# A decoder trunk on one core: attention's written order laid out anew, rsqrt in eleven steps, products by twos

## The chip, the cores and the metric

The kernel runs on one core of a Trainium2 chip. The metric is the device time of one execution in microseconds (us); for a set of runs the median is given. The engines are TensorE (matmuls, called PE in the profile, its weight loads PEld), VectorE (DVE), ScalarE (ACT), GpSimd (POOL) and SyncE (SP), which issues the DMAs. Each engine works through its own queue in order and waits for others by semaphores.

## The reference, cut to what matters

A trunk of two layers on 256 tokens with a model width of 1024, all in float32. `ffn` is a SwiGLU of hidden width 2816, `rms` an RMS norm:

```python
h = h + 0.5 * ffn(rms(h)); h = h + short_conv(rms(h)); h = h + 0.5 * ffn(rms(h))   # layer 0
k_c, v_c, k_s, v_s, k_w, v_w = shared_kv(h)                                       # one K/V for layer 1
h = h + 0.5 * ffn(rms(h)); h = h + nsa(rms(h), kv); h = h + 0.5 * ffn(rms(h))      # layer 1

def nsa(x):                              # 16 heads of 64 in 4 groups
    q = rms(x @ w_q)                     # per head: q / sqrt(mean(q*q) + 1e-6)
    g = sigmoid(x @ w_g)                 # three gates per head
    # softmax attention over compressed blocks, selected blocks and a window
    return (g0 * o_compressed + g1 * o_selected + g2 * o_window) @ w_o
```

## The kernel before, in words

Activations lie transposed: 1024 features as 8 chunks of 128 partitions, 256 tokens along the free dimension. To keep float32 accuracy every weight tile and every activation is split into a high part and a low remainder in the type fp32r. ACT makes the high part by a copy (L148, "uh" in attention), DVE or POOL the low part by a subtraction (L165, "ul"). A weight block of 128 x 128 then needs two matmuls, which form a pair: the high block against 512 columns (high and low activations side by side; L320 and L429), and the low block against the 256 high columns (L322 and L431). The two halves are added when the result leaves PSUM.

The weights stream through SBUF by DMA in pieces of 128 x 2048. A piece is two units, a unit is 8 blocks. At most six split units are ahead of TensorE.

**FFN, first half** (`ffn_in`): 22 groups of hidden features; in each, gate and up are 8 pairs each, 16 pairs in all. **FFN, second half** (`out_proj`): 8 output columns of 22 pairs each. The order of the pairs is set by a run length: with run r, TensorE does r high products, then their r low products, and so on. `RUNS = (1, 2, 4, 8)` gives group f the run length RUNS[f % 4], and likewise column c; the convolution's groups (24 pairs), the first group of an FFN that has to wait for its norm, and the attention's output projection use run 1.

**Attention** has 16 heads, worked on as 8 pairs of heads p. Its instructions are issued in an order written out by hand: `ORDER` is a list of words, each the name of an operation, with the engine behind a colon where there is a choice (D is DVE, A is ACT, P is POOL). The words are issued from left to right, each engine takes its own in that order, and the order between engines is only what data and buffers ask for. The words that matter here:

- `qHT.k` are the query matmuls of half H of the heads and tile T of the tokens, six matmuls each (L810 to L812). `qsq`, `qsum`, `qrec` make the inverse RMS per head: for H = 0 by a square root on ACT and a reciprocal on DVE, for H = 1 by an iteration without a square root (`q_newton`, L842 to L855), one word with 19 small instructions on 128 x 8 elements. `qrr` multiplies in the token's scale (L860), `qnrm` normalizes the query (DVE, L866), `qtr` transposes it (TensorE, L875), `qput` puts it back into SBUF.
- `S0p`, `S0cp`, `S1p` are the scores of pair p. They take banks of PSUM from a ring of two (tag "mm"). `A0`, `M0`, `U0`, `A1`, `E1` add the bias, take the extreme value and the exponential with its sum, `R` and `W` make the factor (L1026, L1029), `N0` and `N1` multiply it in (POOL, L1032 and L1036, 128 x 512 each), `X` transposes the result (L1045), `C` copies it to SBUF, `PV` multiplies by the values, `Oh` and `Ol` split the output. `cmn` to `cC` are the same for the compressed blocks of two pairs of heads.
- `woC.k` are pieces of the output projection for chunk C (L1186 calls `a_pass`), `wv` adds it to the residual (DVE, L1194), `nh` and `nl` write the high and the low half of the next FFN's input (ACT L268, DVE L272), `ns` squares the chunk and adds it up for the next norm, both on POOL (L285, L288, L289).

A word `uh` that finds no free unit, and a word `ul` that finds no high part waiting, issues nothing.

Of the kernel before, what the change touches and what calls it, by code (L numbers as in the profile page):

```python
# [37 lines left out]
ORDER = """
    q00.0 q00.1 q00.2 norm_pe q00.3 norm_act:A q01.0 norm_dve:D qsq00:A qsum00:D q01.1 uh6:A qsqrt00:A ul6:D q01.2 uh7:A qrec00:D ul7:D qrr00:P q01.3
    uh8:A qnrm00:D gates_pe qsq01:A ul8:D qsum01:D cb0:P qtr00 gates_sum:D qsqrt01:A q10.0 qput00:A cb1:P qrec01:D qrr01:P qnrm01:D cb2:P gates_mm S00  # L40
    gates_exp:A qtr01 cb3:P A00:D q10.1 qput01:D cb4:P M00:D S0c0 cb5:P gates_end:D U00:A S10 cb6:P cx0:D q10.2 A100:D cb7:P A101:D E100:A q10.3 E101:A
    S01 S0c1 qsq10:A A01:D S11 R0:D cx1:D W0:P qsum10:D q11.0 N00:P M01:D qrec10:P cmn0:D U01:A A110:D X00 S02 C00:D S0c2 q11.1 A111:D E110:A cx2:D A02:D
    S12 E111:A N101:P M02:D q11.2 A120:D N100:P U02:A R1:D A121:D qrr10:P X10 csub0:P X20 W1:P qnrm10:D q11.3 N01:P cexp0:A C20:A csum0:D C10:D E120:A
    N110:P crec0:D qtr10 X01 qsq11:A cg0:P qput10:D S03 N111:P C01:A qsum11:D S0c3 E121:A S13 cx3:D cmul0:P A03:D qrec11:P cT0 cmn1:D uh9:A M03:D X21 X11
    cC0:D C21:A S05 R2:D ul9:D C11:A PV0 U03:A A05:D A130:D W2:P qrr11:P PV1 N121:P qnrm11:D Oh0:A E130:A N120:P A131:D qtr11 Ol0:D Oh1:A N02:P X12 E131:A
    M05:D X22 Ol1:D csub1:P S04 qput11:D C12:A X02 R3:D C22:A A04:D W3:P S0c4 N130:P C02:A S0c5 cx4:D M04:D cexp1:A S15 U05:A N131:P cx5:D csum1:D cmn2:D
    S14 crec1:D A150:D cg1:P N03:P X23 U04:A A140:D X13 csub2:P X03 A151:D cmul1:P cT1 A141:D S06 C23:A cC1:A S0c6 C03:D C13:A S16 E141:A cx6:D A06:D PV2
    M06:D E140:A A160:D D06:P PV3 E150:A R4:D A161:D W4:P N141:P cexp2:A Oh2:A csum2:D S07 E151:A N140:P Ol2:D crec2:D S17 A07:D N04:P Oh3:A R5:D M07:D
    X14 E06:A S0c7 E160:A Ol3:D cg2:P X04 W5:P C14:D cmul2:P X24 N05:P cx7:D C04:A U06:D cT2 wo0.0 C24:A cC2:D N151:P cmn3:D E161:A A170:D PV4 N150:P
    A171:D uh10:A csub3:P R6:D E170:A X25 ul10:D W6:P D07:P X05 X15 C25:A C05:D N06:P wo1.0 uh11:A C15:D N161:P X06 cexp3:A ul11:D E07:A PV5 C06:A N160:P  # L50
    Oh4:A csum3:D U07:D E171:A Ol4:D X26 crec3:D cg3:P X16 Oh5:A R7:D C26:D uh12:A cmul3:P wo2.0 W7:P Ol5:D N170:P C16:D uh13:A cT3 wo1.1 ul12:D N171:P
    cC3:A uh14:A wo0.1 ul13:D N07:P X17 ul14:P X27 C17:A X07 C27:D PV6 C07:A PV7 Oh6:A Ol6:D wo0.2 Oh7:A wo2.1 Ol7:D wo0.3 wo2.2 wv0:D uh15:A wo2.3 wo1.2
    wv2:D wo1.3 ns0:P nh0:A wo3.0 uh16:A ul15:P nl0:D wv1:D wo4.0 nh2:A uh17:A ul16:D ns1:P wo3.1 nh1:A nl2:D wo3.2 ul17:D wo3.3 ns2:P wo5.0 uh18:A wv3:D
    wo4.1 ul18:P uh19:A nl1:D wo4.2 nh3:A ul19:D wo4.3 wo5.1 uh20:A ns3:P nl3:D wo5.2 wv4:D uh21:A wo5.3 ul20:P wo6.0 wv5:D nh4:A uh22:A ul21:D wo7.0
    ns4:P nh5:A wo7.1 nl4:D nl5:D ul22:D wo6.1 ns5:P wo6.2 wo6.3 wo7.2 wv6:D wo7.3 wv7:D ns6:P nh6:A nl6:D nh7:A nl7:D ns7:P
"""


# [1 line left out]
def trunk(ctx, tc, A, out):  # L60
# [199 lines left out]
    class Norm:  # L260
# [22 lines left out]
        def square(self, c):  # L283
            if c == 0:
                po.tensor_tensor(out=self.sq, in0=h[c], in1=h[c], op=ALU.mult)  # L285
            else:
# [2 lines left out]
                po.tensor_tensor(out=self.sq, in0=self.sq, in1=s, op=ALU.add)  # L289
# [24 lines left out]

    def a_pass(o, u, xs, ks, last=7, run=1):

        ks = list(ks)
        for i in range(0, len(ks), run):
            for k in ks[i:i + run]:
                pe.matmul(o, u[0][:, k * P:(k + 1) * P], xs[k], start=(k == 0), stop=False)  # L320
            for k in ks[i:i + run]:
                pe.matmul(o[:, :T], u[1][:, k * P:(k + 1) * P], xs[k][:, :T], start=False, stop=(k == last))  # L322
# [458 lines left out]
    X = {}  # L781
# [57 lines left out]
            ve.reciprocal(X["r", hf, tt], s)  # L839
        return fn  # L840

    def q_newton(hf, tt):  # L842
        def fn(e):
            s = X["s", hf, tt]
            y, z = sm([P, 8]), sm([P, 8])
            e.tensor_scalar(out=s, in0=s, scalar1=1.0 / 64, scalar2=EPS, op0=ALU.mult, op1=ALU.add)
            e.tensor_scalar(out=y.bitcast(I32), in0=s.bitcast(I32), scalar1=-0.5, scalar2=float(0x5f3759df), op0=ALU.mult, op1=ALU.add)
            e.tensor_scalar(out=s, in0=s, scalar1=-0.5, scalar2=None, op0=ALU.mult)
            for _ in range(4):
# [3 lines left out]
                e.tensor_tensor(out=y, in0=y, in1=z, op=ALU.mult)  # L853
            X["r", hf, tt] = y
        return fn  # L855

    def q_rr(hf, tt):
        def fn(e):
            r = X["r", hf, tt]
            e.tensor_scalar(out=r, in0=r, scalar1=rq[:, tt:tt + 1], scalar2=None, op0=ALU.mult)  # L860
# [426 lines left out]
```

## Time and profile before

| | |
|---|---|
| median of 3 runs | 1000.1 us |
| the three runs | 997.15, 1000.1, 1002.04 us |
| the profiled execution | 997.46 us |
| its span, first to last instruction | 995.7 us |
| mean granted TensorE clock | 0.998 |
| busy in the span | PE 979.1, DVE 742.6, ACT 558.1, POOL 188.2 us |
| attention, first query matmul to the rows matmul of the last FFN | 703.0 to 811.8 us |
| the other stages begin at | FFN 6, its projection 136, convolution 198, FFN 288, its projection 413, shared K/V 475, FFN 509, its projection 641; after attention the last FFN, its projection 930 |

Times in the profile count from the start of the span. A row of the timeline gives the start, the length, the engine, the line, the operation with output and inputs, the count, and in brackets how long the engine had been idle and what ended that. A row of a group gives, behind the bar, the busy time in us and the mean length of one instruction in ns, then the idle time before them and what ended it. Matmuls overlap in TensorE's pipeline, so their lengths add up to more than the time between their starts.

### The profile page before, as it was taken

To read this page: it belongs to the slowest core of one execution; us is meant where nothing else is said; L and a number is where in the kernel's file an instruction comes from. 1 tells how busy PE (TensorE), PEld (TensorE's weight loads), DVE (VectorE), ACT (ScalarE), POOL (GpSimd) and SP (SyncE) were. 2 spreads that over 40 slices of the span, in tenths; PEclk is the share of its full clock that TensorE was granted. 3 is DMA by queue.
4 is the path that set the end of the run, shared out by engine and by line. 5 is a ranking of instruction groups with operands and counts; after the bars stand their busy time and mean duration, and the time that the engine had idled before them with its cause. 6 is when DMAs were issued, how large, how long until landed. Compare 5 with 4: busy or idle time off the path is not lost.

```text
span 995.7 us, 14600 instructions
## 1 busy us (share of the span) xinstructions
PE 979.1 (98%) x5672; PEld 840.2 (84%) x5672; DVE 742.6 (75%) x1059; ACT 558.1 (56%) x897; POOL 188.2 (19%) x278
## 2 busy tenths in 40 slices
PE   8999999999999999999999999999998989999998
PEld 6888888888888888888888888888866778888887
DVE  6987775568898787877559988866568798787752
ACT  4766554455456655554456667644578556655530
POOL 5000001134460000011011031011368750000000
PEclk9999999999999999999999999999999999999999
DMA  7755565545645655555634556564800445555550
GB/s 241 257 184 200 176 212 182 199 133 207 201 150 209 198 183 186 201 206 169 201 137 153 192 205 219 204 212 160 254 19 4 152 148 206 197 183 187 200 185 22
DMA packets 28721, 177.59 MB, mean 178 GB/s; under 512 B 3259, under 2 KB 6587, under 8 KB 7916
## 3 DMA queue, kind: packets, MB, share of 16 engines
q1 hardware_dynamic: 28652, 176.66, 52.3%
q8 instruction: 44, 0.72, 0.3%
q14 instruction: 25, 0.20, 0.1%
HBM read 175.57 MB, written 1.08 MB: 177 GB/s over the span
## 4 chain that ended last, share of the span: by engine, by line
PE 91%; POOL 4%; DVE 2%; issue 2%; DMA 1%; SPq 0%; ACT 0%; DVEq 0%; POOLq 0%; ACTq 0%
PE mm L320 36%; PE mm L322 18%; PE a L429 17%; PE a L431 9%; PE a L320 2%; POOL pr L1036 1%; PE a L539 1%; PE a L541 1%; PE a L540 1%; PE a L322 1%; DVE xs L272 1%; POOL t L1032 1%; DMA hall<-in_x_dram 1%; DVE wl L165 1%; DVE hall L1194 1%
## 5 line engine op out<-in xcount | busy, mean ns | idle before, releaser
L320 PE MATMUL mm<-xs,wh 128*128 128x512 f32 x1536 | 474.5, 398 | 5.3 <-DVE xs L272 2.8
L165 DVE TENSOR_TENSOR wl<-ws,wh 128x1024 fp32r<-128x1024 f32 x318 | 399.1, 1258 | 84.8 <-ACT wh L148 73.2
L148 ACT CAST wh<-ws 128x1024 fp32r<-128x1024 f32 x322 | 335.7, 1045 | 85.8 <-PE a L429 60.2
L322 PE MATMUL mm<-xs,wl 128*128 128x256 f32 x1536 | 316.9, 281 | 0.8 <-DVE wl L459 0.8
L320 PEld LDWEIGHTS mm<-xs,wh 128*128 128x128 f32 x1536 | 268.0, 189 | 49.7 <-DVE xs L279 3.9
L322 PEld LDWEIGHTS mm<-xs,wl 128*128 128x128 f32 x1536 | 262.1, 189 | 28.1 <-DVE wl L459 1.3
L429 PE MATMUL a<-act,wh 128*128 128x512 f32 x722 | 216.5, 395 | 0.0
L431 PE MATMUL a<-act,wl 128*128 128x256 f32 x722 | 141.7, 280 | 0.0
L429 PEld LDWEIGHTS a<-act,wh 128*128 128x128 f32 x722 | 124.2, 188 | 17.7
L431 PEld LDWEIGHTS a<-act,wl 128*128 128x128 f32 x722 | 121.5, 189 | 14.3
L332 DVE TENSOR_TENSOR t<-mm,t 128x512 f32<-128x512 f32 x96 | 66.1, 688 | 76.7 <-ACT t L331 76.1
L331 ACT COPY t<-mm 128x512 f32<-128x512 f32 x96 | 56.1, 584 | 102.9 <-PE mm L322 102.9
L347 ACT ACTIVATE t<-t 128x256 f32<-128x256 f32 x88 | 36.8, 419 | 63.7 <-DVE t L336 63.6
L336 DVE TENSOR_TENSOR t<-t,R 128x512 f32<-128x512 f32 x88 | 61.6, 700 | 2.8
L288 POOL TENSOR_TENSOR t<-hall 128x256 f32<-128x256 f32 x42 | 35.6, 847 | 137.6 <-DVE hall L398 128.6
L285 POOL TENSOR_TENSOR sq<-hall 128x256 f32<-128x256 f32 x6 | 3.7, 615 | 301.5 <-DVE hall L398 294.8
L325 ACT CAST act<-t 128x256 fp32r<-128x256 f32 x96 | 39.0, 407 | 28.3 <-DVE t L493 19.3
L278 ACT ACTIVATE xs<-hall,gains 128x256 fp32r<-128x256 f32 x40 | 19.7, 505 | 53.9 <-DVE hall L398 49.9
L398 DVE SCALAR_TENSOR_TENSOR hall<-a,hall 128x256 f32<-128x256 f32 x78 | 32.9, 422 | 17.9 <-PE a L431 14.9
L326 DVE TENSOR_TENSOR act<-t,act 128x256 fp32r<-128x256 f32 x96 | 41.0, 427 | 4.3 <-ACT act L325 4.3
L348 DVE TENSOR_TENSOR t<-t,t 128x256 f32<-128x256 f32 x88 | 36.9, 420 | 4.0 <-ACT t L347 4.0
L279 DVE SCALAR_TENSOR_TENSOR xs<-hall,gains,xs 128x256 fp32r<-128x256 f32 x40 | 27.1, 687 | 15.7 <-ACT xs L278 15.7
(233 smaller groups left out, 837.5 us busy)
## 6 DMA issues: line engine op xcount, KB each, us to landing
ws<-in_ffn_w_in_dram SPq DMA_DIRECT2D x86, 1024.0 KB, 4.9
ws<-in_ffn_w_out_dram SPq DMA_DIRECT2D x44, 1024.0 KB, 4.8
ws<-in_conv_w_in_dram SPq DMA_DIRECT2D x12, 1024.0 KB, 4.7
ws<-in_w_kv_dram SPq DMA_DIRECT2D x6, 1024.0 KB, 4.9
ws<-in_conv_w_out_dram SPq DMA_DIRECT2D x4, 1024.0 KB, 4.8
ws<-in_attn_w_q_dram SPq DMA_DIRECT2D x4, 1024.0 KB, 4.8
ws<-in_attn_w_o_dram SPq DMA_DIRECT2D x4, 1024.0 KB, 9.8
...
```

Source lines behind the costliest of these rows:

```text
L148: ac.copy(h, src)
L165: e.tensor_tensor(out=l, in0=src, in1=h.bitcast(F32), op=ALU.subtract)
L320: pe.matmul(o, u[0][:, k * P:(k + 1) * P], xs[k], start=(k == 0), stop=False)
L322: pe.matmul(o[:, :T], u[1][:, k * P:(k + 1) * P], xs[k][:, :T], start=False, stop=(k == last))
L325: ac.copy(dst[:, :T], src)
L326: ve.tensor_tensor(out=dst[:, T:], in0=src, in1=dst[:, :T].bitcast(F32), op=ALU.subtract)
L331: ac.copy(r, o[:, :, T:])
L332: ve.tensor_tensor(out=r, in0=o[:, :, :T], in1=r, op=ALU.add)
L336: ve.tensor_tensor(out=r, in0=r, in1=R[:, None, :].to_broadcast([P, n, T]), op=ALU.mult)
L348: ve.tensor_tensor(out=s, in0=s, in1=r[:, 1], op=ALU.mult)
L429: pe.matmul(o, wh, lhs[k], start=(k == 0), stop=False)
L431: pe.matmul(o[:, :T], wl, lhs[k][:, :T], start=False, stop=(k == n - 1))
```

## The change

1. `RUNS = (2, 2, 2, 2)`, and the default run length of `a_pass` and `a_group` is 2.
2. The iteration for the queries of the second half is rewritten. It works on half the mean square, so that a step is z = y*y, z = z*s, y = (z - 1.5)*y, whose sign flips each time; three rounds are done instead of four, which gives 11 instructions instead of 19. The sign is undone in `qrr`. Each instruction is a word of its own, `qnt1T.i`, with an engine of its own.
3. `ns` is divided: `nq` squares on ACT, `ns` adds on POOL (seven of them, the first square is written in place).
4. `ORDER` is laid out anew, with the lengths of operations taken from a trace. The engine changes in 19 words: all `ul` words are now on DVE (four were on POOL), `qrr10` goes from POOL to DVE, and of the copies `C` and `cC` seven go from DVE to ACT and seven from ACT to DVE.
5. The buffer of the compressed scores of two pairs is made by whichever of the two comes first (`cx`).

```diff
-    RUNS = (1, 2, 4, 8)
-    def a_pass(o, u, xs, ks, last=7, run=1):
+    RUNS = (2, 2, 2, 2)
+    def a_pass(o, u, xs, ks, last=7, run=2):
...
-    def a_group(parts, xs, mid=None, run=1):
+    def a_group(parts, xs, mid=None, run=2):
...
+        def square_by_act(self, c):
+            self.s = getattr(self, "s", {})
+            o = self.sq if c == 0 else t1()
+            ac.activation(o, h[c], AF.Square)
+            self.s[c] = o
+        def add(self, c):
+            po.tensor_tensor(out=self.sq, in0=self.sq, in1=self.s.pop(c), op=ALU.add)
...
-    def q_newton(hf, tt):
+    def q_newton(hf, tt, i):
         def fn(e):
             s = X["s", hf, tt]
...
+            if i == 0:
+                e.tensor_scalar(out=s, in0=s, scalar1=0.5 / 64, scalar2=0.5 * EPS, op0=ALU.mult, op1=ALU.add)
+            elif i == 1:
+                e.tensor_scalar(out=y.bitcast(I32), in0=s.bitcast(I32), scalar1=-0.5, scalar2=float(0x5f3759df - (1 << 22)),
+                                op0=ALU.mult, op1=ALU.add)
+            elif i % 3 == 2:
                 e.tensor_tensor(out=z, in0=y, in1=y, op=ALU.mult)
+            elif i % 3 == 0:
                 e.tensor_tensor(out=z, in0=z, in1=s, op=ALU.mult)
-                e.tensor_scalar(out=z, in0=z, scalar1=1.5, scalar2=None, op0=ALU.add)
-                e.tensor_tensor(out=y, in0=y, in1=z, op=ALU.mult)
-            X["r", hf, tt] = y
+            else:
+                e.scalar_tensor_tensor(out=y, in0=z, scalar=1.5, in1=y, op0=ALU.subtract, op1=ALU.mult)
```

The new list, in the stretch of the first iteration, in that of the second, at the last pairs, and at the end:

```
... A02:D W1:P E101:A N01:P qsum10:D S12 cx2:D E100:A N110:P qnt10.0:D M02:D qnt10.1:D q11.1 U02:A qnt10.2:D R0:D N111:P qnt10.3:D
A120:D qnt10.4:D A121:D W0:P qnt10.5:P q11.2 N100:P E120:A qnt10.6:D qnt10.7:D qnt10.8:D qnt10.9:D N101:P E121:A qnt10.10:D q11.3
qrr10:D qnrm10:D N00:P R2:D qtr10 qsq11:A W2:P cT0 N02:P qput10:D X20 cC0:A S03 qsum11:D C20:A N121:P S05 uh9:A A03:D S0c3 X10
qnt11.0:D N120:P cx3:D M03:D uh10:A X00 S13 C10:D qnt11.1:P C00:A qnt11.2:P cmn1:D qnt11.3:P A05:D csub1:P U03:A X11 qnt11.4:D
A130:D PV0 qnt11.5:P qnt11.6:P qnt11.7:D C11:D qnt11.8:P cexp1:A qnt11.9:P E130:A csum1:D qnt11.10:D A131:D qrr11:P X01 Oh0:A X21
qnrm11:D uh11:A S04 C01:D qtr11 ...
... N170:P wo0.1 cmul3:P ul12:D X17 wo1.1 C17:A N07:P cT3 X27 ul14:D cC3:A X07 C27:A PV6 C07:A ul11:D ul13:D PV7 ...
... wo7.0 nl5:D uh22:A wv6:D ns4:P wo7.1 ul18:D nq6:A nh6:A wo7.2 wo7.3 ns5:P wv7:D ns6:P nq7:A nl6:D nh7:A ns7:P nl7:D ul20:D ul21:D ul22:D
```

More of the change, by code (lines that the diff above doesn't have):

```diff
@@ L38 @@
 ORDER = """
[L39 to L54, printed above, removed]
@@ new lines @@
+    U01:A csub0:P S10 A110:D q10.3 cexp0:A A111:D E110:A csum0:D A100:D E111:A S02 crec0:D A101:D cg0:P S0c2 cmul0:P qsq10:A q11.0 R1:D A02:D W1:P E101:A
+    N01:P qsum10:D S12 cx2:D E100:A N110:P qnt10.0:D M02:D qnt10.1:D q11.1 U02:A qnt10.2:D R0:D N111:P qnt10.3:D A120:D qnt10.4:D A121:D W0:P qnt10.5:P
+    q11.2 N100:P E120:A qnt10.6:D qnt10.7:D qnt10.8:D qnt10.9:D N101:P E121:A qnt10.10:D q11.3 qrr10:D qnrm10:D N00:P R2:D qtr10 qsq11:A W2:P cT0 N02:P
+    qput10:D X20 cC0:A S03 qsum11:D C20:A N121:P S05 uh9:A A03:D S0c3 X10 qnt11.0:D N120:P cx3:D M03:D uh10:A X00 S13 C10:D qnt11.1:P C00:A qnt11.2:P
@@ new lines @@
+    S06 Oh2:A Ol3:D E151:A S0c6 Ol2:D S16 cg2:P A06:D N140:P R5:D X04 M06:D cmul2:P X24 cx6:D C04:A A160:D W5:P X14 D06:P C24:A S07 A161:D C14:A S0c7
+    N05:P E06:A cT2 A07:D S17 E161:A cC2:D N151:P U06:D PV4 E160:A M07:D N150:P cx7:D A170:D uh14:A D07:P R6:D A171:D X05 Oh4:A X15 E170:A Ol4:D W6:P
+    N06:P X25 C05:D wo0.0 C15:A C25:D N161:P E07:A cmn3:D PV5 E171:A U07:D N160:P R7:D W7:P ul10:D csub3:P X16 Oh5:A cexp3:A X26 C16:A N171:P Ol5:D X06
+    C26:A csum3:D wo1.0 crec3:D C06:D cg3:P N170:P wo0.1 cmul3:P ul12:D X17 wo1.1 C17:A N07:P cT3 X27 ul14:D cC3:A X07 C27:A PV6 C07:A ul11:D ul13:D PV7
@@ new lines @@
+    Oh6:A Ol6:D wo1.2 Oh7:A wo0.2 Ol7:D wo2.0 wo1.3 wo0.3 wv1:D uh15:A wo3.0 wv0:D nq1:A wo3.1 nh1:A ul15:D uh16:A wo4.0 nq0:A nl1:D nh0:A ns1:P wo4.1
+    nl0:D wo4.2 ul16:D wo3.2 wo3.3 wo4.3 wv3:D uh17:A wo2.1 wv4:D nq3:A wo2.2 nh3:A wo2.3 ul17:D uh18:A wo5.0 nq4:A wv2:D uh19:A wo6.0 nl3:D nq2:A wo5.1
+    ul19:D nh2:A nh4:A uh20:A wo5.2 nl4:D wo5.3 ns2:P wo6.1 wv5:D uh21:A ns3:P wo6.2 nh5:A wo6.3 nl2:D nq5:A wo7.0 nl5:D uh22:A wv6:D ns4:P wo7.1 ul18:D
+    nq6:A nh6:A wo7.2 wo7.3 ns5:P wv7:D ns6:P nq7:A nl6:D nh7:A ns7:P nl7:D ul20:D ul21:D ul22:D
@@ L840, in q_rec @@
         return fn
-    def q_newton(hf, tt):
+    def q_newton(hf, tt, i):
         def fn(e):
             s = X["s", hf, tt]
[L845 to L849, printed above, removed]
+            if i == 0:
+                X["y", tt], X["z", tt] = sm([P, 8]), sm([P, 8])
+            y, z = X["y", tt], X["z", tt]
+            if i == 0:
+                e.tensor_scalar(out=s, in0=s, scalar1=0.5 / 64, scalar2=0.5 * EPS, op0=ALU.mult, op1=ALU.add)
[3 more added lines that the diff above has]
+            elif i % 3 == 2:
                 e.tensor_tensor(out=z, in0=y, in1=y, op=ALU.mult)
+            elif i % 3 == 0:
                 e.tensor_tensor(out=z, in0=z, in1=s, op=ALU.mult)
-                e.tensor_scalar(out=z, in0=z, scalar1=1.5, scalar2=None, op0=ALU.add)
-                e.tensor_tensor(out=y, in0=y, in1=z, op=ALU.mult)
-            X["r", hf, tt] = y
+            else:
+                e.scalar_tensor_tensor(out=y, in0=z, scalar=1.5, in1=y, op0=ALU.subtract, op1=ALU.mult)
         return fn
@@ L858, in fn @@
         def fn(e):
-            r = X["r", hf, tt]
-            e.tensor_scalar(out=r, in0=r, scalar1=rq[:, tt:tt + 1], scalar2=None, op0=ALU.mult)
+            if hf:
+                r = X["r", hf, tt] = sm([P, 8])
+                e.tensor_scalar(out=r, in0=X["y", tt], scalar1=rq[:, tt:tt + 1], scalar2=-1.0, op0=ALU.mult, op1=ALU.mult)
+            else:
+                r = X["r", hf, tt]
+                e.tensor_scalar(out=r, in0=r, scalar1=rq[:, tt:tt + 1], scalar2=None, op0=ALU.mult)
         return fn
@@ L903, in trunk @@
             else:
-                add(f"qrec{n}", q_newton(hf, tt))
+                for i in range(11):
+                    add(f"qnt{n}.{i}", q_newton(hf, tt, i))
             add(f"qrr{n}", q_rr(hf, tt))
@@ L1077, in cx @@
         def cx(e):
-            if i2 == 0:
+            if ("cm", m) not in X:
                 X["cm", m] = mk([P, 2, 2, 2, 16], "cm", 2)
@@ L1205, in trunk @@
         add(f"nl{c}", lambda e, c=c: nm2.low(c))
-        add(f"ns{c}", lambda e, c=c: nm2.square(c))
+        add(f"nq{c}", lambda e, c=c: nm2.square_by_act(c))
+        if c:
+            add(f"ns{c}", lambda e, c=c: nm2.add(c))
     W.limit, W.cap = NBUF, 1 << 20
```

8 lines of the change are left out of this document (7 added, 1 removed).

## The prediction

> **What bounds the kernel now.** I read the page's chain that ended last first, then the busy time of each engine stage by stage (the rows with two times: length, then PE, weight loads, DVE, ACT and POOL), then TensorE's timeline, and last the rows of the engines that it waits for.
>
> ```profile
> PE 91%; POOL 4%; DVE 2%; issue 2%; DMA 1%; SPq 0%; ACT 0%; DVEq 0%; POOLq 0%; ACTq 0%
> ...
> 785.10:802.80 17.70, 17.43 (x100) 15.01 (x99) 15.18 (x20) 9.08 (x13) 13.33 (x10) 1.00 0.42 147
> 802.80:811.80 9.00, 6.20 (x33) 4.53 (x31) 8.82 (x11) 4.18 (x5) 8.23 (x9) 1.00 0.44 157
> 703.00:811.80 108.80, 99.73 (x681) 75.58 (x679) 83.33 (x196) 69.81 (x184) 76.45 (x137) 1.00 0.36 113
> ```
>
> TensorE's matmuls are 91% of the chain, so outside attention only a shorter matmul stream can help. Attention, from the first query matmul at 703.0 to the rows matmul of the last FFN at 811.8, is the exception: TensorE is idle 108.80 - 99.73 = 9.07 us there, 2.8 of them in the last 9 us. These are its five waits above one microsecond:
>
> ```profile
> 736.10 1.09 PE L1045 MATMUL a<-small,pr 128*128 128x128 f32 x8 [1.78 <-POOL pr L1036]
> ...
> 748.39 0.63 PE L875 MATMUL a<-small,t 128*128 128x128 f32 x4 [1.68 <-DVE t L866]
> ...
> 780.83 0.66 PE L1045 MATMUL a<-small,t 128*128 128x128 f32 x4 [1.10 <-POOL t L1032]
> ...
> 805.46 0.47 PE L320 MATMUL mm<-xs,wh 128*128 128x512 f32 x1 [1.10 <-DVE xs L272]
> ...
> 808.36 0.50 PE L320 MATMUL mm<-xs,wh 128*128 128x512 f32 x1 [1.50 <-DVE xs L272]
> ```
>
> Together 7.16 us; 1.91 lie in smaller ones. The first three end when POOL lets something go (the second through DVE, which had waited for the query scale of POOL), the last two when DVE writes a low half of the normalized input.
>
> **Part 1, runs of two.** All groups now take two high products, then two low ones. The price is read where nothing else moves, between group starts of the first FFN, and between output columns:
>
> ```profile
> 90.92 0.40 PE L320 MATMUL mm<-xs,wh 128*128 128x512 f32 x1
> 96.54 0.40 PE L320 MATMUL mm<-xs,wh 128*128 128x512 f32 x1
> ...
> 124.56 0.40 PE L320 MATMUL mm<-xs,wh 128*128 128x512 f32 x1
> 130.22 0.40 PE L320 MATMUL mm<-xs,wh 128*128 128x512 f32 x1
> 135.81 0.40 PE L429 MATMUL a<-act,wh 128*128 128x512 f32 x1
> 143.58 0.40 PE L429 MATMUL a<-act,wh 128*128 128x512 f32 x1
> 151.26 0.40 PE L429 MATMUL a<-act,wh 128*128 128x512 f32 x1
> 158.96 0.40 PE L429 MATMUL a<-act,wh 128*128 128x512 f32 x1
> 166.62 0.40 PE L429 MATMUL a<-act,wh 128*128 128x512 f32 x1
> ...
> 212.02 0.40 PE L320 MATMUL a<-xs,wh 128*128 128x512 f32 x1
> 220.50 0.40 PE L320 MATMUL a<-xs,wh 128*128 128x512 f32 x1
> ```
>
> Columns of 22 pairs take 7.77, 7.68, 7.70 and 7.66 us at runs of 1, 2, 4 and 8: 0.09 in four, eight columns in three projections (0.54) and seven in the last (0.2). Groups of 16 pairs take 5.66 us at run 1 (from 124.56), 5.59 at run 2 (130.22) and 5.62 at run 4 (90.92); run 8 by the columns is 7.66 x 16 / 22 = 5.57. Four groups gain 0.07 + 0.03 - 0.02 = 0.08; an FFN has 22, so 0.45, and four FFNs 1.8. A convolution group has 24 pairs at run 1, 8.48 us; at 5.59 / 16 a pair it is 8.39, eight times 0.09 = 0.7. The short projections of convolution and attention have about 50 pairs that join a run of two, at 0.07 / 16 each: 0.2. Sum **-3.4 us**. TensorE is busy all through these stages, so nothing hides it.
>
> The Trainium skill ("TensorE: Matmul & The Clock Gate", sections "LDWEIGHTS (loading the stationary operand)" and "Back-to-back issue gap") gives 128 / 1.2 = 107 ns for a weight load and 256 / 2.4 + 2.5 = 109 ns for the shorter matmul. By it every load is hidden in any order and this term would be zero; the trace disagrees, by the differences above.
>
> **Part 2, the rsqrt iteration.** Before, one word puts 19 dependent steps on POOL in one block, twice.
>
> ```profile
> 728.67 0.20 POOL L846 TENSOR_SCALAR sm<-sm 128x8 f32<-128x8 f32 x1
> ...
> 733.84 0.20 POOL L853 TENSOR_TENSOR sm<-sm,sm 128x8 f32<-128x8 f32 x1
> 734.00 2.04 POOL L1036 TENSOR_TENSOR pr<-pr,sm 128x512 f32<-128x512 f32 x2
> ...
> 740.89 0.20 POOL L846 TENSOR_SCALAR sm<-sm 128x8 f32<-128x8 f32 x1
> ...
> 742.54 1.03 POOL L853 TENSOR_TENSOR sm<-sm,sm 128x8 f32<-128x8 f32 x1
> ...
> 746.86 0.20 POOL L853 TENSOR_TENSOR sm<-sm,sm 128x8 f32<-128x8 f32 x1
> ...
> 742.34 1.17 DVE L165 TENSOR_TENSOR wl<-ws,wh 128x1024 fp32r<-128x1024 f32 x1
> ```
>
> The first holds POOL's queue 5.4 us (18 spacings of 0.287), and the products that X10 waits 1.78 us for stand right behind it; the second holds it 6.2 us, and the 1.68 is behind that one. Now there are 11 steps, in the first chain ten on DVE and one on POOL, in the second four and seven. POOL loses 38 steps and gets 8; DVE gets 14 and a scale.
>
> A 128x8 step has no row on DVE. The nearest is the reciprocal of that size, 187 ns (below); POOL's 287 ns is the other end for an undisturbed one. I take 187. But the row at 742.54 shows a third price: a 128x8 POOL step took 1.03 instead of 0.20 while DVE ran a weight split (742.34 to 743.51) that reads two SBUF tiles. The reverse happens at 788.70: DVE's split, 0.48 us alone, ended 0.29 after POOL's.
>
> ```profile
> L1026 DVE RECIPROCAL sm<-sm 128x8 f32<-128x8 f32 x8 | 1.5, 187 | 0.0
> ...
> L866 DVE TENSOR_TENSOR t<-a,sm 128x512 f32<-128x512 f32 x4 | 2.8, 692 | 5.5 <-POOL sm L860 5.5
> L279 DVE SCALAR_TENSOR_TENSOR xs<-hall,gains,xs 128x256 fp32r<-128x256 f32 x1 | 0.5, 483 | 0.6 <-ACT xs L278 0.6
> ...
> 788.70 2.63 DVE L272 SCALAR_TENSOR_TENSOR xs<-hall,gains,xs 128x256 fp32r<-128x256 f32 x1
> ...
> 788.64 2.40 POOL L165 TENSOR_TENSOR wl<-ws,wh 128x1024 fp32r<-128x1024 f32 x1
> ...
> 732.66 0.50 PE L810 MATMUL a<-wh,xs 128*128 128x512 f32 x1
> ...
> 733.92 0.40 PE L812 MATMUL a<-wl,xs 128*128 128x512 f32 x1
> ```
>
> In the new list, after the POOL step of the first chain, TensorE has q11.2 and q11.3 left before the transposes of that query tile: 12 matmuls at (733.92 - 732.66) / 5 = 0.25, 3.0 us. Opposite stand steps 6 to 10 on DVE, while POOL does N100, N101 and N00, 1.02 each, without a gap. Undisturbed: 0.29 + 5 x 0.187 + 0.19 (scale) + 0.69 (normalization) = 2.1, covered with 0.9 to spare. If steps 6, 7 and 8 each wait for one product: 0.29 + 3.06 + 3 x 0.19 + 0.69 = 4.6, **1.6 us of idle TensorE**, and A- and M-words queued behind on DVE are late too. I take the second, since steps 6 to 10 read two SBUF tiles as the split does. The Trainium skill ("SBUF — State Buffer", section "Who interferes with whom") says that such a DVE instruction contends with a GpSimd one that reads SBUF, and the later fully blocks; it names no size below which it doesn't. The trace agrees at 788.70; no run yet shows it for a small DVE step.
>
> In the second chain POOL itself waits for DVE's steps, so no product stands in between: 7 x 0.287 + 4 x 0.187 = 2.8 instead of 6.2. The 1.68 goes.
>
> **Part 3, the other moves.** All weight splits go to DVE, squares of the attention output's norm to ACT; POOL keeps seven adds there.
>
> ```profile
> L165 DVE TENSOR_TENSOR wl<-ws,wh 128x1024 fp32r<-128x1024 f32 x318 | 399.1, 1258 | 84.8 <-ACT wh L148 73.2
> L347 ACT ACTIVATE t<-t 128x256 f32<-128x256 f32 x88 | 36.8, 419 | 63.7 <-DVE t L336 63.6
> ...
> L165 POOL TENSOR_TENSOR wl<-ws,wh 128x1024 fp32r<-128x1024 f32 x4 | 9.8, 2442 | 0.0
> L289 POOL TENSOR_TENSOR sq<-sq,t 128x256 f32<-128x256 f32 x8 | 7.1, 885 | 0.6
> L1194 DVE SCALAR_TENSOR_TENSOR hall<-mm,hall 128x256 f32<-128x256 f32 x8 | 3.3, 420 | 1.3 <-PE mm L322 1.1
> ...
> 778.76 2.02 POOL L1032 TENSOR_TENSOR t<-t,sm 128x512 f32<-128x512 f32 x1
> ```
>
> POOL loses 9.8 us of splits that held DVE up; DVE gains 4 x 1.26. Squares cost ACT 8 x 0.42 = 3.4 (an activation of the same shape), hidden: ACT is busy 9.08 of 17.70. From the last value products TensorE has 52 pairs of the projection and 14 of the FFN, 66 x 0.349 = 23.0 us, before it needs the last low half; DVE starts 2.4 us in and must do 16 x 0.42 + 8 x 0.48 + 5 x 1.26 = 16.9, so 3.7 to spare. Seven adds of 0.885 that each stop DVE cost 6.2, 2.5 too many. Between 0 and 2.5 I take **1.0 left** of 2.6. X07's 1.10 stays: N07 took 2.02 beside a split, and two splits stand beside it again. Of the 1.91 in small waits, which no edit addresses one by one, I leave 0.8, between 0 and all.
>
> **Sum.** Idle left 1.6 + 1.1 + 1.0 + 0.8 = 4.5 of 9.07: **-4.6**. With the runs -8.0. The profiled execution took 997.46 (span 995.7 and 1.8 around it), which makes 989.5; the median of the three runs is 1000.1, 2.6 above it, so I forecast **992.1 us**.
>
> **Rivals.** (a) Small DVE steps aren't stopped, and the tail's cover holds: 1.9 idle left, -10.6, **989.5**. For it: 0.9 to spare. Against: 788.70. (b) The waits only move: each engine's queue is in order, and one late word on DVE delays the scores' evacuation and with it the next scores. Idle again 9, the runs alone, **996.7**. For it: DVE is busy 83 of 108.8 and gets 8 us more. Against: POOL, which ended most waits, loses 9 us of steps (11.6 for 8 x 0.287) and 9.8 of splits. (c) The pair order does nothing: -4.6, **995.5**; against it, columns and groups differ by their run length alone. This is what the rule on weight loads, named above from the Trainium skill, would give. (d) Slower: the mutual stop of DVE and POOL becomes the bound. It lies in the two chains and the tail: 11 two-tile steps of both chains behind 1.02 (11.2), four more splits doubled as at 778.76 (4.2), seven adds (6.2), 21.6 idle instead of 9.07: 1000.1 - 3.4 + 12.5 = **1009**. It decides once idle passes 12.5; against it: in the second chain POOL has nothing else to run.
>
> **How the numbers follow.** My forecast 0.58 (990 to 995), (a) 0.17, (b) 0.17, (c) 0.03, (d) 0.05. A difference below 0.5%, 5 us, can't be told from none here. Faster: forecast and (a), and a third of (b), 0.80; same 0.15; slower 0.05. The range reaches from no idle left (1000.1 - 3.4 - 9.1 = 987.6) and 2 us of the spread of the runs (997.15 to 1002.04) below it, 985.5, to just past (b), 997.5.
>
> **What would show it.** Right: group starts 5.59 apart in every FFN; no wait of X10 for products; DVE steps near 1 us beside POOL's products, and an idle TensorE of 1 to 2 us before the transposes of the third query tile; TensorE busy over 95% from 703 to 802. Wrong: steps all near 0.19 (then (a)); idle of 9 us at other words, the scores' banks above all (b); groups still unequal (c).

## The result and the profile after

The changed kernel takes **990.77 us** in the median of four runs (990.24 to 991.3), the kernel before 1000.52 (997.15 to 1002.04): a ratio of 0.9907, 95% interval 0.9881 to 0.9933. The two profiled executions, 990.75 and 997.46 us, have spans of 988.9 and 995.7.

The page of the kernel after (span, busy times, chain of waits), then its busy times over attention (first query matmul to rows matmul; columns as in the prediction: PE, weight loads, DVE, ACT, POOL, granted clock, DMA share, GB/s):

```profile
span 988.9 us, 14575 instructions
...
PE 976.5 (99%) x5672; PEld 838.3 (85%) x5672; DVE 745.8 (75%) x1078; ACT 560.3 (57%) x905; POOL 163.8 (17%) x235
...
PE 96%; DVE 2%; POOL 1%; issue 0%; DMA 0%; ACT 0%; SPq 0%; POOLq 0%; DVEq 0%; ACTq 0%
```

```profile
701.01:805.85 104.84, 99.83 (x679) 76.65 (x678) 84.06 (x214) 72.05 (x192) 51.64 (x94) 0.98 0.34 108
```

TensorE's share of the chain has grown from 91% to 96%, POOL's has gone from 4% to 1%. In attention TensorE is idle 104.84 - 99.83 = 5.0 us instead of 9.07, but its clock there is 0.98 and not 1.00: something besides waiting has come in. (In before the rows matmul starts at 811.40; the prediction's window went on to 811.80, with no idle time in between. So attention is 108.41 us long here.) These are TensorE's waits in attention above 0.3 us:

```profile
735.53 1.09 PE L894 MATMUL a<-small,t 128*128 128x128 f32 x4 [2.41 <-DVE sm L1046]
...
739.74 0.40 PE L994 MATMUL mm<-KT,wh 64*128 64x16 f32 x4 [0.34 <-DVE t L1003]
...
775.59 0.33 PE L1172 MATMUL a<-small,zp 128*128 128x128 f32 x1 [0.43 <-POOL zp L1167]
777.56 0.66 PE L1065 MATMUL a<-small,t 128*128 128x128 f32 x4 [1.21 <-POOL t L1052]
790.70 0.73 PE L331 MATMUL mm<-act,wh 128*128 128x512 f32 x2 [0.62 <-DVE hall L1214]
```

The first is `qtr10`, the transposes of the third query tile. They read `t`, which the normalization (L885) has written by 735.38; the reciprocal that the profile names stands right behind it in DVE's queue. The 1.21 is `X07`; the last is the second piece of the output projection of chunk 2, which waits for `wv3` to have read its PSUM bank. Of before's five large waits only X07's is left. No wait for a low half (`xs`) remains at the tail.

Stage by stage, between the rows matmuls that follow each norm's squares (and the first query matmul), in us of the two profiled spans:

| stage | before | after | difference |
|---|---|---|---|
| start to first rows matmul | 20.40 | 22.15 | +1.75 |
| FFN 1 and its projection | 184.47 | 183.55 | -0.92 |
| convolution | 89.33 | 88.25 | -1.09 |
| FFN 2, projection, shared K/V | 214.33 | 213.27 | -1.06 |
| first FFN of layer 1 to the first query matmul | 194.45 | 193.79 | -0.66 |
| attention | 108.41 | 104.84 | -3.57 |
| last FFN to the end | 184.27 | 183.10 | -1.17 |

### The profile page after: what moved, and what is told of

Read it like the earlier page. It is cut to its first block, busy times and chain, and to the rows that moved or that the text cites. A ratio compares the mean times of both kernels' runs of the same rounds, so it can differ in the third digit from the quotient of the medians.

```text
span 988.9 us, 14575 instructions
## 1 busy us (share of the span) xinstructions
PE 976.5 (99%) x5672; PEld 838.3 (85%) x5672; DVE 745.8 (75%) x1078; ACT 560.3 (57%) x905; POOL 163.8 (17%) x235
## 4 chain that ended last, share of the span: by engine, by line
PE 96%; DVE 2%; POOL 1%; issue 0%; DMA 0%; ACT 0%; SPq 0%; POOLq 0%; DVEq 0%; ACTq 0%
PE mm L331 37%; PE mm L333 18%; PE a L440 17%; PE a L442 8%; PE a L331 3%; PE a L333 1%; PE a L550 1%; PE a L552 1%; PE a L551 1%; PE a L1065 1%; PE a L821 1%; PE mm L999 1%; PE a L1081 1%; PE a L822 1%; PE a L823 1%; PE mm L990 0%
## 5 line engine op out<-in xcount | busy, mean ns | idle before, releaser
L331 PE MATMUL mm<-xs,wh 128*128 128x512 f32 x1536 | 488.5, 399 | 2.7 <-DVE xs L281 2.2
L333 PEld LDWEIGHTS mm<-xs,wl 128*128 128x128 f32 x1536 | 289.6, 189 | 69.1 <-DVE wl L470 0.8
L333 PE MATMUL mm<-xs,wl 128*128 128x256 f32 x1536 | 304.2, 279 | 0.5 <-DVE wl L470 0.5
L331 PEld LDWEIGHTS mm<-xs,wh 128*128 128x128 f32 x1536 | 235.8, 189 | 5.7 <-DVE xs L281 4.3
L440 PE MATMUL a<-act,wh 128*128 128x512 f32 x722 | 226.7, 395 | 0.0
L442 PEld LDWEIGHTS a<-act,wl 128*128 128x128 f32 x722 | 135.6, 188 | 32.1
L440 PEld LDWEIGHTS a<-act,wh 128*128 128x128 f32 x722 | 109.9, 189 | 0.0
L290 POOL TENSOR_TENSOR t<-hall 128x256 f32<-128x256 f32 x35 | 27.4, 783 | 134.8 <-DVE hall L409 134.6
```

What stands on the lines that cost most here:

```text
L440: pe.matmul(o, wh, lhs[k], start=(k == 0), stop=False)
L442: pe.matmul(o[:, :T], wl, lhs[k][:, :T], start=False, stop=(k == n - 1))
```

## The experiments

Attention's length in the profile of each run, in the order of the text, with TensorE's idle time in it and the parts of it at half clock:

| kernel | run times, median (us) | attention (us) | idle (us) | half clock in attention (us) |
|---|---|---|---|---|
| before | 1000.52 | 108.41 | 9.07 | none |
| after | 990.77 | 104.84 | 5.0 | 3.41 |
| e2_runs_alone | 995.57 | 109.83 | 8.9 | 3.41 |
| e4_order_alone | 995.10 | 103.63 | 5.0 | none |
| e3_scale_on_pool | 987.19 | 101.91 | 2.9 | none |
| e1_start_run1 | 988.93 | 106.12 | 4.7 | 6.83 |
| e6_best_run2 | 985.24 | 99.82 | 1.2 | none |
| e5_best_run1 | 984.48 | 99.84 | 1.2 | none |
| e7_splits_on_pool | 991.05 | 105.46 | 5.3 | 3.41 |
| e8_squares_on_pool | 989.27 | 103.59 | 5.2 | none |
| e9_splits_squares_on_pool | 992.72 | 109.19 | 7.5 | 6.83 |

Each was compared with the kernel before on its own chip: e1 to e4 with 1000.37, e5 to e8 with 999.42, e9 with 1000.19.

### The two parts alone

```diff
  e2: before, with
-    RUNS = (1, 2, 4, 8)            # and run=1 in a_pass and a_group
+    RUNS = (2, 2, 2, 2)            # and run=2
  e4: after, with
-    RUNS = (2, 2, 2, 2)            # and run=2
+    RUNS = (1, 2, 4, 8)            # and run=1
```

> The kernel before with the run lengths of two alone. Theory 'more than the columns showed': between the traces all stages outside attention and the start gained 4.9 us, because a group of run two that follows another of run two is shorter than one that follows a run of one; with the 1.75 us lost at the start the time is 1000.5 - 4.9 + 1.75 = 997.4, and an FFN's groups of 16 pairs are 5.57 apart. Rival 'the prediction's price': 3.4 us and the same loss, 998.9, groups 5.59 apart. Rival 'the loss at the start is not of the runs': 995.6.

> The changed kernel with the old run lengths (1, 2, 4, 8, and 1 as the default): list, rsqrt steps and divided squares alone. Theory 'the parts add up': attention gains its 3.6 us, the start has its short half clock again, all other stages are as before: 1000.5 - 3.6 = 996.9. Rival 'the list needs the shorter runs' (attention's projection is in runs of two there): less than 2 us of gain, 998.5 or more.

Runs of two alone give 995.57 us, ratio 0.9944 (0.9926 to 0.9963); the new list alone 995.10, 0.9939 (0.991 to 0.9968). Against 1000.37 that is -4.8 and -5.3, -10.1 together, and both together gave 990.77 - 1000.52 = -9.7: within the spread of the runs the parts add up. In e2's profile every stage but the start and attention is shorter by nearly what it is shorter by in the kernel after (-0.90, -1.06, -1.05, -0.66, -1.07, together -4.7); in e4's these stages stand within 0.13 of before. So the column of differences above, attention and start left out, is the pair order but for some 0.1 in the last stage: **-4.90 us**.

The starts of TensorE's doubled matmuls in the kernel after, two in an FFN group and two in a column of the projection:

```profile
84.11 0.63 PE L331 MATMUL mm<-xs,wh 128*128 128x512 f32 x2
...
95.95 0.63 PE L331 MATMUL mm<-xs,wh 128*128 128x512 f32 x2
...
137.06 0.63 PE L440 MATMUL a<-act,wh 128*128 128x512 f32 x2
...
144.72 0.63 PE L440 MATMUL a<-act,wh 128*128 128x512 f32 x2
```

Between the first two lie 17 double pairs: (95.95 - 84.11) / 17 = 0.6965 us, so a group of 8 double pairs takes 5.57 and a column of 11 takes 7.66, which is 144.72 - 137.06.

### The query scale on POOL: what the 2.41 us are

The chain of the third query tile in the kernel after, its steps on DVE and the instructions of POOL beside them:

```profile
730.53 0.16 DVE L869 SCALAR_TENSOR_TENSOR sm<-sm,sm 128x8 f32<-128x8 f32 x1
...
731.29 0.70 DVE L867 TENSOR_TENSOR sm<-sm,sm 128x8 f32<-128x8 f32 x1
732.03 0.96 DVE L869 SCALAR_TENSOR_TENSOR sm<-sm,sm 128x8 f32<-128x8 f32 x1
733.02 0.96 DVE L865 TENSOR_TENSOR sm<-sm 128x8 f32<-128x8 f32 x1
734.02 0.17 DVE L867 TENSOR_TENSOR sm<-sm,sm 128x8 f32<-128x8 f32 x1
734.22 0.17 DVE L869 SCALAR_TENSOR_TENSOR sm<-sm,sm 128x8 f32<-128x8 f32 x1
734.42 0.23 DVE L876 TENSOR_SCALAR sm<-sm,rc 128x8 f32<-128x8 f32 x1
734.69 0.69 DVE L885 TENSOR_TENSOR t<-a,sm 128x512 f32<-128x512 f32 x1
```

```profile
730.77 0.20 POOL L865 TENSOR_TENSOR sm<-sm 128x8 f32<-128x8 f32 x1 [0.64 <-DVE sm L869]
730.93 2.04 POOL L1056 TENSOR_TENSOR pr<-pr,sm 128x512 f32<-128x512 f32 x2
732.93 1.04 POOL L1052 TENSOR_TENSOR t<-t,sm 128x512 f32<-128x512 f32 x1
```

A step on 128 x 8 takes 0.16 to 0.17 us when POOL is still, and 0.70, 0.96 and 0.96 while POOL runs its three products without a gap (730.93 to 733.97): one step gets through for each product. The first step after POOL's last product takes 0.17 again. One of the three (733.02) reads a single tile through both inputs and is stopped as well.

To show that this is the cause and not the length of the chain, e3 takes POOL's products out of the chain's way. The step after the chain, `qrr10`, goes to POOL, which makes POOL wait for the chain before it starts the products; nothing of the computation changes:

```diff
-  W0:P qnt10.5:P q11.2 N100:P E120:A qnt10.6:D ... N101:P E121:A qnt10.10:D q11.3 qrr10:D qnrm10:D N00:P R2:D qtr10
+  W0:P qnt10.5:P q11.2 E120:A qnt10.6:D ... E121:A qnt10.10:D qrr10:P qnrm10:D N100:P N101:P N00:P q11.3 R2:D qtr10
-  ... qput10:D X20 cC0:A S03 qsum11:D C20:A N121:P S05 uh9:A
+  ... qput10:D cC0:A S03 qsum11:D N121:P S05 X20 C20:A uh9:A
```

> The changed kernel with the scale behind the first rsqrt chain (qrr10) on POOL instead of DVE and put ahead of N100, N101 and N00 in POOL's queue, so that POOL has nothing to run beside steps 6 to 10 on DVE; X20 with its copy C20 is moved behind S05, since its product comes later. Theory 'stopped by POOL': steps 7 and 8, which took 0.96 us each, take 0.2; TensorE's 2.41 us before the transposes of the third query tile shrink below 0.5, and the half clock of 3.4 us that follows it goes too (half of 3.4): attention is 2.0 + 1.7 = 3.7 us shorter, time 987.1. Rival 'the clock drops for another reason' (the transposes): only 2.0, time 988.8, with the half clock still there. Rival 'the chain is slow by itself' (hops between engines): steps stay near 1 us and the time at 990.8.

Measured 987.19 us (986.82 to 987.88), ratio 0.986 (0.9827 to 0.9892). The last steps of the chain on DVE, the scale and the products on POOL, and the transposes, in e3:

```profile
730.31 0.16 DVE L868 TENSOR_TENSOR sm<-sm,sm 128x8 f32<-128x8 f32 x1
730.51 0.17 DVE L870 SCALAR_TENSOR_TENSOR sm<-sm,sm 128x8 f32<-128x8 f32 x1
730.71 0.17 DVE L866 TENSOR_TENSOR sm<-sm 128x8 f32<-128x8 f32 x1
...
731.69 0.69 DVE L886 TENSOR_TENSOR t<-a,sm 128x512 f32<-128x512 f32 x1 [0.41 <-POOL sm L877]
```

```profile
731.38 0.28 POOL L877 TENSOR_SCALAR sm<-sm,rc 128x8 f32<-128x8 f32 x1 [1.38 <-DVE sm L870]
731.61 2.04 POOL L1057 TENSOR_TENSOR pr<-pr,sm 128x512 f32<-128x512 f32 x2
```

```profile
732.53 0.63 PE L895 MATMUL a<-small,t 128*128 128x128 f32 x4 [0.39 <-DVE sm L1047]
```

The same steps take 0.16 to 0.17 us each, and TensorE's wait before the transposes falls from 2.41 to 0.39. Counted from the first query matmul (700.03 in e3, 701.01 in the kernel after) POOL begins its products at 31.58 instead of 29.92, 1.66 later, and TensorE does not wait for them. Attention gets shorter by 104.84 - 101.91 = 2.93 us, more than the 2.0 of the wait, and the half clock is gone.

### Where the half clock comes from

In all profiles the stretches at half clock begin and end on a grid of 3.413 us, fixed by the first of them: in the kernel after 735.24 - 11.61 = 723.63 = 212.0 x 3.413. On that grid, busy times around the large wait (PE busy is the second number, the granted clock the third from the end), first after, then before, e4, e2 and e9:

```profile
731.82:735.24 3.42, 1.30 (x6) 0.75 (x4) 3.21 (x7) 1.25 (x4) 2.15 (x3) 1.00 0.00 0
735.24:738.65 3.41, 3.12 (x14) 2.71 (x16) 1.59 (x4) 1.09 (x3) 3.00 (x4) 0.50 0.00 0
```

```profile
745.31:748.72 3.41, 1.73 (x25) 1.38 (x22) 1.17 (x4) 1.55 (x7) 2.93 (x10) 1.00 0.00 0
748.72:752.13 3.41, 2.65 (x21) 1.65 (x19) 2.92 (x8) 2.24 (x7) 3.18 (x5) 1.00 0.00 0
```

```profile
734.26:737.67 3.41, 2.12 (x10) 1.42 (x8) 3.27 (x9) 2.10 (x7) 2.99 (x3) 1.00 0.00 0
737.67:741.08 3.41, 2.27 (x18) 1.76 (x18) 2.64 (x7) 1.32 (x3) 2.15 (x3) 1.00 0.00 0
```

```profile
743.35:746.76 3.41, 1.18 (x15) 0.72 (x10) 2.02 (x7) 1.55 (x7) 3.16 (x9) 1.00 0.00 0
746.76:750.17 3.41, 3.40 (x14) 2.37 (x15) 1.56 (x5) 1.31 (x4) 3.18 (x5) 0.50 0.00 0
```

```profile
789.70:793.11 3.41, 1.46 (x9) 1.17 (x8) 3.34 (x6) 2.15 (x3) 1.28 (x3) 1.00 0.35 60
793.11:796.52 3.41, 3.41 (x13) 2.83 (x12) 2.72 (x5) 2.08 (x4) 2.18 (x3) 0.50 0.61 252
```

Kernel after: TensorE is idle 3.42 - 1.30 = 2.12 us in one window of the grid, and the next is at half clock. In e4 the very same wait (2.43) falls across a border of the grid, 1.29 and 1.14, and the clock stays. In before the 1.68 lies whole in one window and is not enough; in e2 the same wait and one of 0.56 make 2.23 in one window, and it is. Over the eleven profiles, from the first query matmul to the rows matmul of the last FFN, all six windows with 1.95 us of idle or more (2.42 in e1, 2.32 and 1.95 in e9, 2.28 in e7, 2.23 in e2, 2.12 in after) are followed by half clock, and none with 1.68 or less is; the border lies between, near half a window. Where the grid lies against the kernel differs from profile to profile, so **the same wait costs a clock window in one profile and not in another**. That this also holds from execution to execution of one kernel is suggested by e8's four runs, 987.76 and 988.07 us at a mean clock of 0.998 and 0.996, 990.48 and 990.69 at 0.994; which of their windows were at half clock is not known but for the one profiled.

The end of the span fits the border: windows with 1.95 us or more of idle there (before, after, e1, e2, e3, e5, e6, e8) are followed by half clock, those with 1.62, 1.42 and 1.24 (e7, e4, e9) are not. The start does not: TensorE is idle 1.06 us of e6's window 6.04 to 9.46, and half clock follows; it is idle 1.22 of before's window 4.62 to 8.03, and none does. So idle time in a window isn't the whole rule.

What one window costs is the difference of profiles with the same waits: after, with one, 104.84; e4 and e8, with none, 103.63 and 103.59; e1, with two, 106.12. That is about 1.25 us a window. (e2, with one, against before, with none, gives 1.42.) It is less than the 1.7 us that half of 3.41 would be; why was not tried (waits that would have come anyway may lie under it).

The Trainium skill ("TensorE: Matmul & The Clock Gate", section "What's actually happening") says that the window is free-running and 3413 ns long; the trace agrees (212.0 windows between 11.61 and 735.24). By the Trainium skill ("TensorE: Matmul & The Clock Gate", section "HAM oscillation — how this bites in real kernels") only idle gaps above some 3.4 us matter; the measurement differs, and decides: 1.95 us within one window sufficed.

### The start

In its profile the kernel after loses 1.75 us before its first rows matmul. There the first FFN group, which waits for its norm, changed from run 1 to run 2; e1 gives it run 1 again:

```diff
-                a_pass(o[:, 0], u[0], xs, range(8))
+                a_pass(o[:, 0], u[0], xs, range(8), run=1 if f == 0 else 2)
```

> The changed kernel with one thing undone: in the very first group of the first FFN the pairs go one high, one low again (run 1); all else is as in the changed kernel. Theory 'order at the start': with runs of two the second high product stands before the first low one, so TensorE waits for the next chunk of x in the middle of a stretch in which it runs at half clock; the half clock then lasts 6.8 us instead of 3.4. Undone, the first rows matmul comes back from 22.15 to about 20.4 us and the half clock at the start lasts 3.4 us: the span is 988.9 - 1.75 = 987.2, the time 989.0. Rival 'chance of the window': the longer half clock is a matter of when the execution starts; then the span stays at 988.9 and the half clock at 6.8 us, time 990.8.

Measured 988.93 us (987.87 to 990.0), ratio 0.9875 (0.9846 to 0.9904). Its start is 0.68 shorter than before's, which looked as if the order mattered there. That does not follow: e5 has the same edit and its start is 0.86 longer than before's, e8 has run 2 and its start is exactly as long as before's (20.40). What goes with the length is the half clock at the start, which lasts one window in before, e1 and e8 (19.73 to 20.40 us) and two in all others (20.88 to 22.15). The first two windows of the kernel after, and of before:

```profile
11.61:15.02 3.41, 3.26 (x9) 2.06 (x10) 3.41 (x5) 1.70 (x2) 3.25 (x5) 0.50 0.54 154
15.02:18.44 3.42, 3.42 (x12) 2.84 (x12) 3.42 (x3) 0.29 (x1) 3.15 (x3) 0.50 0.41 86
```

```profile
11.44:14.86 3.42, 3.42 (x9) 2.32 (x9) 3.42 (x5) 1.99 (x3) 3.26 (x5) 0.50 0.55 161
14.86:18.27 3.41, 3.41 (x20) 2.93 (x20) 3.41 (x4) 1.07 (x2) 3.25 (x4) 1.00 0.41 89
```

In before TensorE is busy through the whole first window and the second runs at full clock; in the kernel after 0.15 us of it are idle, and the second is at half clock too. At the start all profiles with 0.15 or more idle there have two half windows, all with 0.09 or less have one. In attention this does not hold (after returned to full clock with 0.29 idle in its half window, e1 stayed at half with none), so what ends a half clock stays open. The +1.75 is that of one profiled execution. With run 1 in the first group two profiles have one half window (before, e1) and two have two (e4, e5); with run 2 one has one (e8) and six have two. So neither order settles it; whether the order shifts the odds is not shown.

### A version with fewer waits

e6 is e3 with four more words moved: the splits `ul14`, `ul11`, `ul13`, which stood beside POOL's last products, go behind them, and `wo5.0` goes ahead of `wv3`, to fill the wait at 790.70. e5 is e6 with e1's edit.

```diff
-  cT3 X27 ul14:D cC3:A X07 C27:A PV6 C07:A ul11:D ul13:D PV7 Oh6:A Ol6:D wo1.2 Oh7:A wo0.2 Ol7:D wo2.0 ... wv0:D
+  cT3 X27 cC3:A X07 C27:A PV6 C07:A PV7 Oh6:A Ol6:D ul14:D wo1.2 Oh7:A wo0.2 Ol7:D ul11:D wo2.0 ... wv0:D ul13:D
-  wo4.3 wv3:D uh17:A wo2.1 ... uh18:A wo5.0
+  wo4.3 wo5.0 wv3:D uh17:A wo2.1 ... uh18:A
```

> As e5, with the first group in runs of two as in the changed kernel. Theory 'a split beside a product': N07 takes 1.04 again instead of 2.02, the waits of 0.43 (cT3) and 1.21 (X07) go, and the 0.62 of wo2.1, which waits for a bank that wv3 still reads, is covered by wo5.0: 987.2 - 2.3 = 984.9. Rival 'they come back at the end': DVE has two more splits behind the last value products, and TensorE waits for the low halves of the last FFN's input instead; then less than 1 us is left of it, 986.2 or more.

> All in one: the scale on POOL ahead of the three products (as before in e3), the three weight splits that stand beside N07 and cmul3 moved behind Ol6, Ol7 and wv0 on DVE, wo5.0 moved ahead of wo2.1, and the first group of the first FFN with run 1. Beside e6, which differs in the first group alone. Theory 'order at the start': with run 1 the half clock at the start lasts one window of 3.4 us, with run 2 two: clock 0.998 against 0.997, and 1.7 us less than e6: 983.2. Rival 'chance of the window': both kernels have executions with one and with two; the medians differ by less than 1 us.

e6: 985.24 us (984.51 to 985.91), ratio 0.9865 (0.9846 to 0.9885). e5: 984.48 (984.4 to 984.85), 0.9859 (0.984 to 0.9877). Both are faster than before, and their runs lie below all runs of the kernel after; the ratio's interval of e6 just overlaps with that of the kernel after (0.9881 to 0.9933), that of e5 does not. TensorE's waits in e6 from the first query matmul on (what waits, for whom, us in all, times, longest):

```profile
PE mm L332 <- DVE hall L1215: 0.6, 1, 0.6
PE a L895 <- DVE sm L1047: 0.4, 1, 0.4
PE mm L991 <- DVE sm L1032: 0.2, 1, 0.2
```

X07's wait and that of the compressed block ahead of it are gone: with no split beside it the product it waits for took 1.03 us instead of 2.02. The wait for `wv3` stays at 0.6, so moving one piece of the projection ahead of it did not cover it; that part of the expectation was wrong. The rows show why: `ul13`, moved behind `wv0`, now stands ahead of `wv3` on DVE. Two splits follow `wv0` (779.94, 2.35 us) where there was one (786.10, 1.22), and `wv3` comes 6.28 us after `wv1` instead of 5.24. That 1.04 is as much as the moved piece (three pairs, 3 x 0.35) gives TensorE to do. No run with `ul13` elsewhere was made. The two versions differ by 0.8 us with overlapping intervals, and their attention is equal: no verdict between them.

### Splits and squares back on POOL

The prediction had 1.6 of the tail's 2.6 us go because splits and squares leave POOL. e7 puts the four splits back, e8 the squares, e9 both, in the new list.

```diff
-  ul14:D ... ul15:D ... ul18:D ... ul20:D
+  ul14:P ... ul15:P ... ul18:P ... ul20:P                       # e7, e9
-            ac.activation(o, h[c], AF.Square)
+            po.tensor_tensor(out=o, in0=h[c], in1=h[c], op=ALU.mult)   # e8, e9
```

> The changed kernel with four weight splits (ul14, ul15, ul18, ul20) back on POOL. Theory 'stopped by POOL': they take 2.4 us each there, and DVE's low halves (two SBUF inputs) wait for them, so the mean of these goes from 0.5 to over 1 us and TensorE waits at the end of attention for 2 to 2.6 us as in the kernel before: 993. Rival 'cover': the list has room for them, within 0.5 us of 990.8.

> The changed kernel with the eight squares of the attention output's norm back on POOL, behind the same words. Theory 'stopped by POOL': eight more POOL instructions of 0.6 to 1.0 us stand beside DVE's splits and low halves, DVE had some 2.5 us to spare, so TensorE waits 1 to 2 us more before the last FFN: 992. Rival 'cover': they lie in POOL's idle time, within 0.5 us of 990.8.

> The kernel after, with its list, but with both of the moves of Part 3 taken back together: the four weight splits that went to DVE (ul14, ul15, ul18, ul20) and the squares of the attention output's norm are on POOL again. Alone, the splits back on POOL gave 991.05 us and 105.46 us of attention, the squares back on POOL 989.27 and 103.59 (no half-clock window there). Theory 'the two moves together make the tail's gain': POOL has splits of 2.4 us and squares of 0.8 in one queue again, DVE's low halves come late, waits for xs of 1 us or more return at the last wo pairs or the first pairs of the FFN, 2 to 2.6 us in all; time 992.5 to 994. Theory 'the order of the list makes it': the same words in the new order have slack enough on TensorE, no wait for xs above 0.5 us, attention within 1.0 of 104.84 with one half-clock window (103.6 without), time 989 to 992.

e7: 991.05 us (989.64 to 991.22), ratio 0.9919 (0.9896 to 0.9943). e8: 989.27 (987.76 to 990.69), 0.9906 (0.9882 to 0.9929). Each move by itself gives at most 0.6 us (attention 105.46 against 104.84 with one half window each; 103.59 against e4's 103.63 with none). After e8 I held the order of the list to be the cause. e9 corrected that: 992.72 us (991.41 to 994.82), ratio 0.9923 (0.9896 to 0.9949), and attention 109.19. Its waits of TensorE, and DVE and POOL ahead of the one that is new in size:

```profile
PE a L895 <- DVE sm L1047: 2.4, 1, 2.4
PE mm L332 <- DVE hall L1215: 1.9, 1, 1.9
PE a L1066 <- POOL t L1053: 1.2, 1, 1.2
PE a L306 <- POOL sq L301: 1.2, 1, 1.2
```

```profile
785.88 3.39 DVE L275 SCALAR_TENSOR_TENSOR xs<-hall,gains,xs 128x256 fp32r<-128x256 f32 x2
789.20 1.76 DVE L168 TENSOR_TENSOR wl<-ws,wh 128x1024 fp32r<-128x1024 f32 x1
790.88 0.87 DVE L1215 SCALAR_TENSOR_TENSOR hall<-mm,hall 128x256 f32<-128x256 f32 x2
```

```profile
785.83 2.41 POOL L168 TENSOR_TENSOR wl<-ws,wh 128x1024 fp32r<-128x1024 f32 x1
788.18 0.81 POOL L297 TENSOR_TENSOR sq<-hall 128x256 f32<-128x256 f32 x1
789.07 0.80 POOL L301 TENSOR_TENSOR sq<-sq,t 128x256 f32<-128x256 f32 x1
```

A split on POOL (785.83) and a low half on DVE (785.88) begin together. The low half takes 2.64 us instead of 0.48 and ends after the split; the split isn't slowed much (2.41, and 2.36 at 777.23, where DVE does nothing). The low half and its neighbour are done after 3.39, the next split takes 1.76 instead of 1.21, `wv3` comes 90.22 us after the first query matmul instead of 88.75, and the 0.62 is 1.95. At the end the rows matmul waits 1.21 for POOL's last add. The two are 3.16 us in place of 0.62, and the 1.95 brings a second window at half clock: 2.5 of idle and some 1.25 of clock, of the 4.35 us by which attention is longer than in the kernel after; the rest is not assigned. So **in the profiles neither move is needed alone, but one of the two is**: with both sets on POOL the slack is used up. The medians alone don't settle it, since the ratios of e9 and of the kernel after overlap; but at a mean clock of 0.993 to 0.994 e9 took 993.73 and 994.82 us, and the kernel after 990.24 to 991.3. Neither theory had the place: the waits are not for low halves.

## Why the prediction was right, and where it was not

**Result.** 992.1 was forecast, 990.77 came, inside the forecast's own 990 to 995 and past the 0.5% that can be told. The number alone does not tell the forecast from rival (a), whose 989.5 is as near. Of the rivals, (a) fell by the steps at 0.96 us, (b) by the idle time of 5.0 instead of 9, (c) by e2, (d) by the same 5.0.

**Part 1** was right in kind and mis-sized: -3.4 forecast, -4.9 measured (attention left out). The term that was mis-sized is the price of a pair in runs of two. In three of the four FFNs the group starts of before lie, by the median, 5.65, 5.59, 5.61 and 5.59 us apart at runs of 1, 2, 4 and 8, and the columns 7.77, 7.68, 7.70 and 7.67. Where all have run 2 they lie 5.57 and 7.66 apart, and the convolution's groups 8.36 instead of 8.48; the forecast had carried over 5.59, 7.68 and 8.39, and had put run 8 at 5.57. By stage the FFNs' first halves gave 2.4 us where 1.8 were forecast, the projections 1.4 where 0.74 were, and the convolution 1.1 where 0.7 and a part of the 0.2 were. In the first FFN of layer 1 other matmuls stand among the pairs, and most groups take 5.6 to 6.3 in both kernels. Why a run of two is shorter among its like was not tried. The rule by which order would not matter (rival c) is refuted by the stages of e2.

**Part 2** named the mechanism and the place: steps 6, 7 and 8 stopped by N100, N101 and N00, and idle TensorE ahead of the third tile's transposes. The length of the chain was right, 4.6 forecast and 735.38 - 730.77 = 4.61 measured from POOL's step to the end of the normalization. The term that was mis-sized is the cover: 3.0 us of query matmuls were counted behind POOL's step, but the last of them stands here:

```profile
732.73 0.39 PE L823 MATMUL a<-wl,xs 128*128 128x512 f32 x1
```

It ends at 733.12, 2.35 after 730.77, so 2.41 us of idle came instead of 1.6: of the twelve query matmuls only nine start behind POOL's step. (The forecast's sign was 1 to 2 us there; and TensorE was busy 93.99 of the 99 us from 703 to 802, 94.9%, just short of the 95% it named.) The Trainium skill's rule of "SBUF — State Buffer", section "Who interferes with whom", of which no run had shown that it holds for a small step, does hold there: 0.96 us instead of 0.17 on 128 x 8, and 0.17 again in e3. The second chain's 1.68 went, as forecast.

**Part 3.** Idle left at the tail was put at 1.0; no wait for a low half is left, but 0.62 stands at 790.70 for `wv3`, a wait the prediction did not have. X07's 1.10 stayed (1.21), for the reason given. Small waits: 0.8 forecast, 0.34 + 0.43 = 0.77 found. The sum of idle left, 4.5, came out at 5.0. The reason given for the tail was half right: by the profiles of e7 and e8 neither the splits nor the squares had to leave POOL, by e9's one of them had to.

**What the sum lacked.** A wait was priced at its own length. The 2.41 also cost a clock window, some 1.25 us, in the profiled execution. Idle -4.06, the window +1.25 and the difference of attention, -3.57, leave -0.76, which is not assigned (the short projections' pair order, put at 0.2 with those of the convolution, is part of it). With the pair order -4.90 and the start +1.75 this is the span's -6.72. And the 2.6 us that were added because the profiled execution of before lay below the median are probably of the same kind: that execution had a clock of 0.998, which no other execution of before on record exceeded; on e1's chip one of 1000.4 us had 0.995, one of 1005.85 had 0.986. The profiled execution of the kernel after (0.994, like the other three at 0.993 to 0.994) already has its half windows in it and lies at the median. So 992.1 was near partly by luck, for a sum of errors that cancel: too high by 1.5 for the pairs, 2.6 for the allowance and the 0.76, too low by 0.5 of idle, 1.25 for the window and 1.75 for the start, which makes some 1.4 in all.
